# Feed-forward second product in seven block products with pre-summed operands, and a Silu gate

## Chip, core and metric

One core of one Trainium2 chip runs the whole block in one launch. The metric is device time in microseconds (us) of that core. The kernel before takes 2396.96 us (median of three runs, 2396.28 to 2398.84). The engines are TensorE (PE; its weight loads are PEld), VectorE (DVE), ScalarE (ACT), GpSimd (POOL) and SyncE (SP), whose queue issues nearly all transfers.

## The reference, cut to what matters

The block computes token mixing with two recurrent branches, a cross-attention into 256 memory tokens, and a SwiGLU feed-forward, on 1024 tokens of width 1024, all in float32. The feed-forward's inner width is 2816.

```python
h = h + (gate_a * y_a + gate_b * y_b) @ w_out[l]
u = rmsnorm(h, norm_xa_g[l])
...
h = h + o @ xa_wo[l]
u = rmsnorm(h, norm_ffn_g[l])
h = h + (jax.nn.silu(u @ ffn_w1[l]) * (u @ ffn_w3[l])) @ ffn_w2[l]
return rmsnorm(h, norm_final_g)
```

The change is about the last product, hidden (1024 x 2816) by ffn_w2 (2816 x 1024), called part two here, and about the silu in the first two products, called part one.

## The kernel before, in words

Every float32 product is made of three matmuls: each operand is split into a rounded high part (an ACT copy, L281) and the remainder (a subtraction on POOL or DVE, L285), and `mm3` (L298 to L301) adds high by high, high by low and low by high into one PSUM tile.

The mixing stage comes first. Then `attention_block` (L1646) runs, in this order: the keys and values, the output projection of the mixing (`add_project` with w_out, L1763), the queries and attention per head (L1830), and the projection with xa_wo (L1846) in two halves of the tokens. `add_project` (L1706) takes the weights in four passes of 256 columns. In a pass it works through steps of two token tiles, 48 matmuls of 256 columns a step; w_out has sixteen steps, each half of xa_wo has eight. Its weights are loaded by `load_w` as four raw tiles a pass and split into six buffers per part (L1648, L1668), so a part of the next pass can only be split while the last step of the pass before is running. After some steps it calls `next(beside)`, which lets a generator add work there.

Part one (L1957 to L2019) is already a seven-product form over halves of the width (1024) and of the inner width. `products(f, A)` runs for f = 0 to 10; each makes two times seven block products (for ffn_w1 and ffn_w3), of 12 matmuls of 512 columns each. `gated` (L1945) gets the two results of one block, first ffn_w1's (n = 0), then ffn_w3's (n = 1): it takes a Sigmoid on ACT and a product on DVE for the first, and a second product on DVE for the second, and stores the 128 x 512 result in the DRAM tensor hid_d, 44 stores in all.

Part two (L2033 to L2098) goes over two halves of the tokens and two halves of the output columns. For each half of the tokens 22 hidden tiles are loaded and split (L2045 to L2047): the first 14 into the ring (names th, tl), the last eight into the tiles ah, al. For each of the four (token half, column half) pairs all 22 tiles of ffn_w2 are loaded and split (names wh, wl), and four accumulators take 22 x 3 matmuls each. The last three steps are run accumulator by accumulator, so that the sums, the squares and the final norm (L2071 to L2098) follow one another. The remainder of the hidden tiles and that of the weights are both taken on POOL.

What sets the order: in the attention and feed-forward stages a scheduler at build time orders each engine's queue by program order as far as a buffer is free and by its own estimate of readiness; in the queue itself the order is fixed. Loads and stores wait on SP in that order.

Of the kernel before, what the change touches and what calls it, by code (L numbers as in the profile page):

```python
# [17 lines left out]
P = 128  # L18
# [165 lines left out]
def tile_trunk(ctx, tc, x, mem, norm_mix_g, w_in, rw_mu, rw_w0, rw_w2, rw_a0, rw_a2, rw_g2,  # L184
# [1454 lines left out]
    early_d = scratch("early_d", [2, HK, P, HALF])  # L1639
    ssq = const.tile([P, 4, 4], F32, name="ssq")  # L1640
# [5 lines left out]
    def attention_block(xctx):  # L1646
# [27 lines left out]
        Kh = kp.tile([P, KT, NM], F32R, name="Kh")  # L1674
        Kl = kp.tile([P, KT, NM], F32R, name="Kl")
        Vh = vp.tile([P, NMT, D], F32R, name="Vh")
        Vl = vp.tile([P, NMT, D], F32R, name="Vl")
# [28 lines left out]
        def add_project(a, w, src, halves, ss=None, beside=iter(())):  # L1706
# [56 lines left out]
        hs = add_project(yT, w_out, x[0], range(NHALF))  # L1763
# [79 lines left out]
        for _ in prev:  # L1843
            pass

        for h in range(NHALF):  # L1846
            hs = add_project(oT, xa_wo, h1d, range(h, h + 1), *((ssq, early_blocks(hs, *fa)) if h else ()))
# [23 lines left out]
    hd = scratch("hid_d", [FT, NHALF, P, HALF])  # L1871
    def raw(src, k, c, kn, cn):
# [20 lines left out]

    def blocks():

        return [[fp.tile([P, HALF], F32, tag=t, name=f"h{t}", bufs=4 if t == "s" else 2) for t in ts] for ts in (("u2", "u3"), ("c", "s"))
                for _ in range(2)]
# [74 lines left out]
    def early_products(f, T1, T4):  # L1972

        for name, T, b in (("P5", T1, "S1"), ("P4", T4, "B22")):
            for n in range(2):
                t = kept[f, name, n] = fp.tile([P, HALF], F32, tag="kept", name=name, bufs=8)
                nc.scalar.activation(t, product(name, T[n], B[b]), AF.Copy)

    def products(f, A):
# [6 lines left out]
        for n in range(2):  # L1986
# [3 lines left out]
            s = gated(n, C, s, f, 1)  # L1990
        for a11, a12, a21, a22 in A:
# [38 lines left out]
    for f in range(HF):  # L2030
        products(f, weights(f))

    fg = fp.tile([P, D], F32, name="fg", bufs=1)  # L2033
    nc.sync.dma_start(out=fg, in_=norm_final_g.partition_broadcast(P))
    order = [f + e for f in range(HF) for e in (0, HF)]
    ILAST = 3
    for h in range(NHALF):
        a = act(act1)
        hid = []
        for n, f in enumerate(order):  # L2040
            if n >= FT - KT:
                hh, hl = (t[:, n - FT + KT, :] for t in a)
            else:
                hh, hl = (ring.tile([P, HALF], F32R, tag=t, name=t) for t in ("th", "tl"))
            nc.sync.dma_start(out=hl.bitcast(F32), in_=hd[f, h])  # L2045
            nc.scalar.activation(hh, hl.bitcast(F32), AF.Copy)
            nc.gpsimd.tensor_tensor(hl, hl.bitcast(F32), hh.bitcast(F32), op=ALU.subtract)  # L2047
            hid.append((hh, hl))
        hs = blocks()
        for i in range(4):  # L2050
            for c in range(2):
                nc.sync.dma_start(out=hs[i][c], in_=h2d[(4 * h + i) * P:(4 * h + i + 1) * P, c * HALF:(c + 1) * HALF])
        ss = sp.tile([P, 4, 8], F32, tag="ssf", name="ssf")
        for c in range(2):
            cs = slice(c * HALF, (c + 1) * HALF)
            acc = [psum("acc") for _ in range(4)]
            w2 = []
            for n, f in enumerate(order):
                w2.append(operand(raw(ffn_w2, f, c * HALF, 1, HALF), "2"))
                if n < FT - ILAST:  # L2060
                    steps = [(i, n) for i in range(4)]
                elif n == FT - 1:
                    steps = [(i, g) for i in range(4) for g in range(FT - ILAST, FT)]
                else:
                    steps = []
                for i, g in steps:
                    ts_ = slice(i * P, (i + 1) * P)
                    mm3(acc[i], hid[g][0][:, ts_], hid[g][1][:, ts_], w2[g][0][:, 0, :], w2[g][1][:, 0, :],
                        g == 0, g == FT - 1)

            sums = []  # L2071

            def finish(i):

                r = ss[:, 3, i:i + 1]
                o1, o2 = hs[i]
                rows = slice((4 * h + i) * P, (4 * h + i + 1) * P)
                nc.scalar.activation(o1, o1, AF.Copy, scale=r)
                nc.sync.dma_start(out=out[rows, 0:HALF], in_=o1)
                ins = nc.vector.scalar_tensor_tensor(o2, o2, r, fg[:, HALF:D], op0=ALU.mult, op1=ALU.mult).ins  # L2080
                behind(ins, sums[-1])
                nc.sync.dma_start(out=out[rows, HALF:D], in_=o2)

            for i in range(4):
                o = hs[i][c]
                r = [ss[:, n, i:i + 1] for n in range(4)]
                sums.append(nc.vector.tensor_tensor(o, acc[i], o, op=ALU.add).ins.name)  # L2087
                junk = sp.tile([P, HALF], mybir.dt.bfloat16, tag="junkf", name="junkf", bufs=2)
                nc.scalar.activation(junk, o, AF.Square, accum_out=r[c])
                if c == 0:  # L2090
                    nc.gpsimd.tensor_tensor(o, o, fg[:, cs], op=ALU.mult)
                    nc.vector.tensor_scalar(r[0], r[0], 1.0 / D, EPS, op0=ALU.mult, op1=ALU.add)
                else:
                    nc.vector.scalar_tensor_tensor(r[2], r[1], 1.0 / D, r[0], op0=ALU.mult, op1=ALU.add)
                    nc.gpsimd.tensor_tensor(r[3], r[2], nhalf[:, 0:1], op=ALU.pow)
                    if i:
                        finish(i - 1)
        finish(3)  # L2098


# [24 lines left out]
```

## Time and profile before

| what | value |
|---|---|
| runs | 2396.28, 2396.96, 2398.84 us |
| the profiled execution's own time | 2398.55 us |
| its span | 2396.8 us |
| TensorE busy | 97% of the span, granted clock 0.99 on average |
| VectorE, ScalarE, GpSimd busy | 59%, 47%, 51% |

Matmuls are pipelined, so a matmul's duration in the trace (0.39 us for 512 columns) is longer than the distance from one start to the next. In the windows a busy share of PE says how much of a stretch was covered, and idle time in front of a matmul is named with what ended it.

### The profile page before, as it was taken

The numbers are of one execution on the slowest core, as the hardware profiler recorded it, in microseconds if no ns is written. First come the engines' busy times: TensorE is split into PE (matmuls) and PEld (weight loads), VectorE is DVE, ScalarE is ACT, GpSimd is POOL, SyncE is SP. The second block draws the span as 40 slices with busy tenths as digits, with TensorE's granted clock in tenths as the row PEclk, the third lists the DMA queues.
The fourth block names the chain that finished last, engine by engine and source line by source line (L and its number), as shares of the span: only waits on it lengthen the run. The fifth ranks groups of instructions, "written<-read, shape, count | busy, mean of one in ns | idle before, by whom it ended". The sixth has DMA issues, their size and how long they took to land. (4 is left out here: it accounts for less than half of the span.)

```text
span 2396.8 us, 48780 instructions
## 1 busy us (share of the span) xinstructions
PE 2335.8 (97%) x19258; PEld 1934.3 (81%) x19258; DVE 1411.2 (59%) x2288; ACT 1128.3 (47%) x2249; POOL 1228.8 (51%) x1268
## 2 busy tenths in 40 slices
PE   7999999999999999999998999999999999999998
PEld 5777777778887878888887998889778888877887
DVE  5887874667777667767754525444687565640101
ACT  6545454646566656555663415444433333343332
POOL 3554545555466555665664511112565444477673
PEclk9999999999999999999999999999999999999999
DMA  5444445333344343434244823133723223265441
GB/s 168 122 127 121 123 117 161 74 101 85 92 109 110 82 129 105 123 89 126 56 140 152 300 69 117 53 120 132 259 80 101 84 75 93 71 199 172 158 161 57
DMA packets 386001, 288.46 MB, mean 120 GB/s; under 512 B 106171, under 2 KB 329517, under 8 KB 385773
## 3 DMA queue, kind: packets, MB, share of 16 engines
q1 hardware_dynamic: 383341, 279.58, 39.6%
q0 software_dynamic: 1344, 4.72, 0.5%
q8 instruction: 152, 2.49, 0.4%
q10 hardware_dynamic: 1088, 1.05, 0.1%
q14 instruction: 76, 0.62, 0.1%
HBM read 208.73 MB, written 76.02 MB: 119 GB/s over the span
## 5 line engine op out<-in xcount | busy, mean ns | idle before, releaser
L102 PE MATMUL pproj<-uh,whi 128*128 128x512 f32 x768 | 320.0, 417 | 1.1 <-DVE q L102 1.1
L102 PE MATMUL pproj<-uh,wlo 128*128 128x512 f32 x768 | 300.9, 392 | 2.8 <-POOL wlo L102 2.1
L102 PE MATMUL pproj<-ul,whi 128*128 128x512 f32 x768 | 301.2, 392 | 0.0
L285 POOL TENSOR_TENSOR wl<-wraw,wh 128x512 fp32r<-128x512 f32 x154 | 202.1, 1323 | 133.2 <-ACT wh L281 131.6
L285 POOL TENSOR_TENSOR wlo<-wraw,whi 128x512 fp32r<-128x512 f32 (+1 forms) x86 | 117.9, 1374 | 288.6 <-ACT whi L281 280.7
L102 POOL TENSOR_TENSOR wlo<-wraw,whi 128x512 fp32r<-128x512 f32 x96 | 129.0, 1355 | 118.8 <-ACT whi L102 103.8
L281 ACT ACTIVATE whi<-wraw 128x512 fp32r<-128x512 f32 (+1 forms) x166 | 101.0, 617 | 173.1 <-PE pw L301 62.0
L299 PE MATMUL pproj<-uh,whi 128*128 128x512 f32 (+1 forms) x432 | 179.5, 416 | 0.9 <-ACT whi L281 0.6
L281 ACT ACTIVATE wh<-wraw 128x512 fp32r<-128x512 f32 x154 | 94.3, 627 | 182.2 <-PE P L300 74.5
L301 PE MATMUL pproj<-uh,wlo 128*128 128x512 f32 (+1 forms) x432 | 171.4, 397 | 1.5 <-POOL wlo L285 1.5
L102 PEld LDWEIGHTS pproj<-uh,whi 128*128 128x128 f32 x768 | 144.4, 188 | 34.3 <-DVE q L102 2.4
L300 PE MATMUL pproj<-ul,whi 128*128 128x512 f32 (+1 forms) x432 | 170.7, 395 | 0.0
L102 PEld LDWEIGHTS pproj<-ul,whi 128*128 128x128 f32 x768 | 144.3, 188 | 32.0
L102 PEld LDWEIGHTS pproj<-uh,wlo 128*128 128x128 f32 x768 | 144.9, 189 | 28.1 <-POOL wlo L102 2.5
L285 POOL TENSOR_TENSOR wlT<-wraw,whT 128x512 fp32r<-128x512 f32 x70 | 96.6, 1386 | 96.2 <-ACT whT L281 92.5
L299 PE MATMUL pw<-whi,ah 128*128 128x256 f32 x512 | 144.6, 282 | 0.0
L300 PE MATMUL pw<-wlo,ah 128*128 128x256 f32 x512 | 144.6, 282 | 0.0
L301 PE MATMUL pw<-whi,al 128*128 128x256 f32 x512 | 144.3, 282 | 0.0
L2087 DVE TENSOR_TENSOR hu<-acc,hu 128x512 f32<-128x512 f32 x8 | 5.5, 692 | 200.0 <-PE acc L301 200.0
L285 DVE TENSOR_TENSOR wlo<-wraw,whi 128x512 fp32r<-128x512 f32 x80 | 73.7, 922 | 83.4 <-ACT whi L281 83.1
L102 ACT ACT_TABLE_LOAD x90 | 115.5, 1283 | 13.5 <-DVE m L102 6.4
L299 PEld LDWEIGHTS pproj<-uh,whi 128*128 128x128 f32 (+1 forms) x432 | 81.6, 189 | 25.4 <-issue 6.2
(457 smaller groups left out, 6656.2 us busy)
## 6 DMA issues: line engine op xcount, KB each, us to landing
wraw<-in_ffn_w_dram SPq DMA_DIRECT2D x192, 256.0 KB
wraw<-in_w_in_dram SPq DMA_DIRECT2D x148, 256.0 KB
hid_d<-s SPq DMA_DIRECT2D x44, 256.0 KB
tok<-in_x_dram SPq DMA_DIRECT2D x16, 512.0 KB
ar_d<-AR SPq DMA_DIRECT2D x32, 256.0 KB
bk_d<-BK SPq DMA_DIRECT2D x16, 512.0 KB
AR<-ar_d SPq DMA_DIRECT2D x64, 128.0 KB
BK<-bk_d SPq DMA_DIRECT2D x16, 512.0 KB
```

The lines of the kernel that those rows point to most:

```text
L102: r = getattr(self.engine, op)(*a, **kw)
L281: nc.scalar.activation(hi, src, AF.Copy)
L285: e.tensor_tensor(lo, src, hi.bitcast(F32), op=ALU.subtract)
L299: nc.tensor.matmul(ps, ah, bh, start=first, stop=False)
L300: nc.tensor.matmul(ps, ah, bl, start=False, stop=False)
L301: nc.tensor.matmul(ps, al, bh, start=False, stop=last)
L2087: sums.append(nc.vector.tensor_tensor(o, acc[i], o, op=ALU.add).ins.name)
```

## The change

The hidden matrix X is cut into X11, X21 (token half 0 and 1, first eleven inner tiles) and X12, X22 (second eleven), ffn_w2 into four blocks Y likewise. Seven block products replace the eight of before; they need four sums of X blocks and four sums of Y blocks.

- The sums of ffn_w2 (`w2_sums`) are made for each of the eleven f in the attention stages: two loads of 512 KB, two subtractions on DVE, two on POOL, one store of 1 MB to wsum_d. Seven f are placed beside the w_out projection, in the buffers of act2, from its third step on; four beside the first half of xa_wo, in the buffers of the keys and values.
- The sums of the hidden blocks (`hidden_sums`) are made in part one: for each f two operations on DVE, two on POOL and four stores to hsum_d. 33 of the 44 hidden tiles are still stored.
- `gated` takes Silu on ACT in place of Sigmoid and a product on DVE. The gate tiles share a ring of 14 with the kept products (before: rings of 4 and 8).
- Part two runs seven blocks of eleven items. An item loads one hidden (or sum) tile and one weight (or sum) tile, eight items ahead, splits both four items ahead (the hidden remainder on DVE, the weight's on POOL), and feeds twelve matmuls. The block results are combined on ACT and DVE. All hidden tiles now go through the ring; the tiles ah, al hold the sixteen residual tiles, loaded at its start.

```diff
+        def w2_sums(fs, places):
...
+            def sums(f, y):
+                y11, y12, y21, y22 = (y[:, n, :] for n in range(4))
+                nc.vector.tensor_tensor(y11, y12, y11, op=ALU.subtract)
+                nc.gpsimd.tensor_tensor(y12, y22, y12, op=ALU.subtract)
+                nc.gpsimd.tensor_tensor(y22, y22, y11, op=ALU.subtract)
+                nc.vector.tensor_tensor(y21, y22, y21, op=ALU.subtract)
+                nc.sync.dma_start(out=wsd[f], in_=y)
+
+            loaded = []
+            for place in places:
+                if place:
+                    y = place()
+                    f = next(fs)
+                    load(f, y)
+                    loaded.append((f, y))
+                    if len(loaded) < 3:
+                        yield
+                        continue
+                if loaded:
+                    sums(*loaded.pop(0))
+                yield
...
-                    if c > 1 or c == 1 and i2 % 2:
+                    if every or c > 1 or c == 1 and i2 % 2:
                         next(beside, None)
...
-        hs = add_project(yT, w_out, x[0], range(NHALF))
+        hs = add_project(yT, w_out, x[0], range(NHALF), every=True, beside=w2_sums(
+            w2f, [None, None] + [in_act2(tag, n) for tag in ("ah", "al", "ah") for n in range(2)] + [in_act2("al", 0)]))
...
+                             **({} if h else dict(beside=w2_sums(w2f, in_kv), every=True)))
...
         if n == 0:
-            s = fp.tile([P, HALF], F32, tag="s", name="s", bufs=4)
-            nc.scalar.activation(s, C, AF.Sigmoid)
+            s = fp.tile([P, HALF], F32, tag="kept", name="s", bufs=14)
+            nc.scalar.activation(s, C, AF.Silu)
+            return s
         nc.vector.tensor_tensor(s, C, s, op=ALU.mult)
         if n:
-            nc.sync.dma_start(out=hd[f, t], in_=s)
+            hid[f, t] = s
+            if (f, t) != (f % HF, 1):
+                nc.sync.dma_start(out=hd[f, t], in_=s)
...
+    def hidden_sums(f):
+        x11, x21, x12, x22 = (hid.pop(k) for k in ((f, 0), (f, 1), (f + HF, 0), (f + HF, 1)))
+        tt(x22, x21, x22, op=ALU.add)
+        nc.gpsimd.tensor_tensor(x21, x11, x21, op=ALU.subtract)
+        tt(x11, x22, x11, op=ALU.subtract)
+        nc.gpsimd.tensor_tensor(x12, x12, x11, op=ALU.subtract)
+        for n, t in enumerate((x22, x11, x21, x12)):
+            nc.sync.dma_start(out=hsd[n, f], in_=t)
...
+        if f:
+            hidden_sums(f - 1)
...
+    hidden_sums(HF - 1)
...
-            nc.gpsimd.tensor_tensor(hl, hl.bitcast(F32), hh.bitcast(F32), op=ALU.subtract)
...
+    ILAST, LOOK, LOADS = 3, 4, 8
+    blocks = ((lambda f: hd[f, 0], w2(0, 0), p1),
+              (lambda f: hd[f + HF, 0], w2(1, 0), lambda i, acc: add(0, i, 0, acc, ALU.add, True)),
+              (lambda f: hsd[1, f], wsum(3), p6),
+              (lambda f: hsd[0, f], wsum(0), p5),
+              (lambda f: hsd[3, f], w2(1, 1), lambda i, acc: add(0, i, 1, acc, ALU.add, False)),
+              (lambda f: hsd[2, f], wsum(1), p7),
+              (lambda f: hd[f + HF, 1], wsum(2), lambda i, acc: add(1, i, 0, acc, ALU.subtract, False)))
...
+    def split_item(b, f):
+        hl, y = loaded.pop((b, f))
+        hh = ring.tile([P, HALF], F32R, tag="th", name="th")
+        nc.scalar.activation(hh, hl.bitcast(F32), AF.Copy)
+        tt(hl, hl.bitcast(F32), hh.bitcast(F32), op=ALU.subtract)
+        ops[b, f] = (hh, hl, *operand(y, "2"))
...
+    for n, (b, f) in enumerate(items):
+        if n + LOADS < len(items):
+            load_item(*items[n + LOADS])
+        if n + LOOK < len(items):
+            split_item(*items[n + LOOK])
```

## Rows read from the trace of the kernel before

**Rows 1.** The page: the span, and part 1, busy time of each engine.
```profile
span 2396.8 us, 48780 instructions
PE 2335.8 (97%) x19258; PEld 1934.3 (81%) x19258; DVE 1411.2 (59%) x2288; ACT 1128.3 (47%) x2249; POOL 1228.8 (51%) x1268
```
**Rows 2.** Windows: stretch, length, busy time (count) per engine, granted clock, DMA share, GB/s.
```profile
1360.00:1454.00 94.00, 93.95 (x784) 93.72 (x782) 32.23 (x52) 23.30 (x41) 21.04 (x15) 1.00 0.39 136
...
1594.00:1644.00 50.00, 49.67 (x407) 48.11 (x406) 20.25 (x37) 15.03 (x29) 9.67 (x7) 1.00 0.49 165
...
1800.00:2139.00 339.00, 339.00 (x1484) 278.47 (x1483) 202.79 (x260) 116.06 (x192) 179.30 (x137) 1.00 0.31 98
2139.00:2200.00 61.00, 54.21 (x231) 42.64 (x230) 13.11 (x12) 19.57 (x35) 46.84 (x37) 1.00 0.64 207
2200.00:2390.00 190.00, 189.84 (x829) 155.59 (x827) 19.38 (x37) 61.06 (x115) 114.33 (x94) 1.00 0.37 120
```
**Rows 3.** Timeline of PE, starts 24 and 33 matmuls apart, in two stretches.
```profile
2133.84 0.39 PE L299 MATMUL P<-hS,wh 128*128 128x512 f32 x1
...
2139.30 0.39 PE L299 MATMUL acc<-wh,th 128*128 128x512 f32 x1
...
2375.03 0.39 PE L299 MATMUL acc<-wh,ah 128*128 128x512 f32 x1
...
2382.71 0.39 PE L299 MATMUL acc<-wh,ah 128*128 128x512 f32 x1
```
**Rows 4.** PE timeline, 2144 to 2185 us: the matmuls that waited, in brackets.
```profile
2144.85 0.50 PE L299 MATMUL acc<-wh,th 128*128 128x512 f32 x1 [3.35 <-DVE C L2010]
...
2164.72 0.51 PE L300 MATMUL acc<-wl,th 128*128 128x512 f32 x1 [1.94 <-POOL wl L285]
...
2168.46 0.50 PE L300 MATMUL acc<-wl,th 128*128 128x512 f32 x1 [0.68 <-POOL wl L285]
...
2183.43 0.50 PE L300 MATMUL acc<-wl,th 128*128 128x512 f32 x1 [0.68 <-POOL wl L285]
```
**Rows 5.** Timelines of DVE and POOL at the turn to part two.
```profile
2137.13 6.47 DVE L1950 TENSOR_TENSOR s<-C,s 128x512 f32<-128x512 f32 x1 [10.19 <-ACT s L1949]
...
2138.04 2.55 POOL L2047 TENSOR_TENSOR tl<-tl,th 128x512 fp32r<-128x512 f32 x2
2140.52 2.52 POOL L285 TENSOR_TENSOR wl<-wraw,wh 128x512 fp32r<-128x512 f32 x2
```
**Rows 6.** Groups, 2139 to 2397 us: busy, mean ns, idle before, releaser.
```profile
L285 POOL TENSOR_TENSOR wl<-wraw,wh 128x512 fp32r<-128x512 f32 x86 | 110.5, 1300 | 47.9 <-ACT wh L281 46.4 <-issue 1.4
...
L281 ACT ACTIVATE wh<-wraw 128x512 fp32r<-128x512 f32 x84 | 51.1, 625 | 90.5 <-PE acc L301 71.9 <-DMA wraw<-in_ffn_w_dram 8.5 <-POOL wl L285 3.9
```
**Rows 7.** Timelines of POOL and DVE, splits at a pass boundary of w_out.
```profile
1382.60 3.01 POOL L285 TENSOR_TENSOR wlo<-wraw,whi 128x512 fp32r<-128x512 f32 x2 [12.68 <-ACT whi L281]
...
1383.22 1.23 DVE L285 TENSOR_TENSOR wlo<-wraw,whi 128x512 fp32r<-128x512 f32 x1 [4.23 <-ACT whi L281]
...
1385.03 1.12 DVE L285 TENSOR_TENSOR wlo<-wraw,whi 128x512 fp32r<-128x512 f32 x1
```
**Rows 8.** Windows of 10 us with much traffic, the same columns as rows 2.
```profile
1370.00:1380.00 10.00, 10.00 (x86) 10.00 (x85) 2.73 (x7) 0.00 (x0) 0.00 (x0) 1.00 0.98 371
2150.00:2160.00 10.00, 9.89 (x44) 7.91 (x43) 3.04 (x3) 6.63 (x13) 6.64 (x6) 1.00 0.88 276
```
**Rows 9.** Groups of part one, 1698 to 2139 us.
```profile
L285 POOL TENSOR_TENSOR wl<-wraw,wh 128x512 fp32r<-128x512 f32 x68 | 91.5, 1352 | 85.3 <-ACT wh L281 85.2
...
L1950 DVE TENSOR_TENSOR s<-C,s 128x512 f32<-128x512 f32 x43 | 47.5, 1106 | 20.4 <-ACT s L1949 19.8
...
L1993 DVE TENSOR_TENSOR T<-wraw 128x512 f32<-128x512 f32 x22 | 20.9, 948 | 41.8 <-POOL wl L285 41.8
...
L1949 ACT ACTIVATE s<-C 128x512 f32<-128x512 f32 x22 | 13.9, 631 | 29.3 <-DVE C L2010 22.8 <-DVE C L1989 6.2 <-DMA wraw<-in_ffn_w_dram 0.3
...
L1949 ACT ACT_TABLE_LOAD x1 | 1.3, 1283 | 0.0
```

More of the change, by code (lines that the diff above doesn't have):

```diff
@@ L1704, in attention_block, with load, add_project @@
             nc.sync.dma_start(out=t[:, 0:KEYS, :].bitcast(F32), in_=kd[n])
-        def add_project(a, w, src, halves, ss=None, beside=iter(())):
+        def w2_sums(fs, places):
+            def load(f, y):
+                for r in range(2):
+                    rows = slice((f + r * HF) * P, (f + r * HF + 1) * P)
+                    nc.sync.dma_start(out=y[:, 2 * r:2 * r + 2, :].rearrange("p c t -> p (c t)"), in_=ffn_w2[0, rows, :])
+            def sums(f, y):
[18 more added lines that the diff above has]
+                yield
+            for l in loaded:
+                sums(*l)
+                yield
+        def add_project(a, w, src, halves, ss=None, beside=iter(()), every=False):
             hs = []
@@ L1844, in attention_block @@
             pass
+        in_kv = [lambda p=p, t=t: p.tile([P, 4, HALF], F32, tag=t, name="y2")
+                 for p, t in ((kp, "Kh"), (kp, "Kl"), (vp, "Vh"), (vp, "Vl"))]
         for h in range(NHALF):
-            hs = add_project(oT, xa_wo, h1d, range(h, h + 1), *((ssq, early_blocks(hs, *fa)) if h else ()))
+            hs = add_project(oT, xa_wo, h1d, range(h, h + 1), *((ssq, early_blocks(hs, *fa)) if h else ()),
+                             **({} if h else dict(beside=w2_sums(w2f, in_kv), every=True)))
             for i in range(4):
@@ new lines, in tile_trunk, with add @@
+    U = [fp.tile([P, HALF], F32, tag=("u2", "u3")[i // 2], name="Uw") for i in range(4)]
+    V = [fp.tile([P, HALF], F32, tag="kept", name="Vw", bufs=14) for i in range(4)]
+    ss = [sp.tile([P, 4, 8], F32, tag="ssf", name="ssf") for _ in range(NHALF)]
+    sums = {}
+    def add(h, i, c, acc, op, first):
+        o = hs[h][:, 2 * i + c, :]
+        r = [ss[h][:, n, i:i + 1] for n in range(4)]
+        sums[h, i] = (nc.vector.tensor_tensor(o, o, acc, op=op) if op == ALU.subtract else tt(o, acc, o, op=op)).ins.name
+        junk = sp.tile([P, HALF], mybir.dt.bfloat16, tag="junkf", name="junkf", bufs=2)
+        nc.scalar.activation(junk, o, AF.Square, accum_out=r[0 if first else 1])
+        if first:
+            nc.gpsimd.tensor_tensor(o, o, fgs[c], op=ALU.mult)
+            nc.vector.tensor_scalar(r[0], r[0], 1.0 / D, EPS, op0=ALU.mult, op1=ALU.add)
+        else:
+            nc.vector.scalar_tensor_tensor(r[2], r[1], 1.0 / D, r[0], op0=ALU.mult, op1=ALU.add)
+            nc.gpsimd.tensor_tensor(r[3], r[2], nhalf[:, 0:1], op=ALU.pow)
+            if i:
+                finish(h, i - 1, c, sums[h, i])
+            if i == 3:
+                finish(h, 3, c, None)
@@ new lines, in finish @@
+    def finish(h, i, c, order):
+        r = ss[h][:, 3, i:i + 1]
+        rows = slice((4 * h + i) * P, (4 * h + i + 1) * P)
+        o1, o2 = hs[h][:, 2 * i + 1 - c, :], hs[h][:, 2 * i + c, :]
+        if h == 0:
+            nc.vector.tensor_scalar(o1, o1, r, None, op0=ALU.mult)
+        else:
+            nc.scalar.activation(o1, o1, AF.Copy, scale=r)
+        nc.sync.dma_start(out=out[rows, (1 - c) * HALF:(2 - c) * HALF], in_=o1)
+        ins = nc.vector.scalar_tensor_tensor(o2, o2, r, fgs[c], op0=ALU.mult, op1=ALU.mult).ins
+        if order:
+            behind(ins, order)
+        nc.sync.dma_start(out=out[rows, c * HALF:(c + 1) * HALF], in_=o2)
@@ new lines, in more, with p1, p6, p5 @@
+    def more(h, i, c, t):
+        o = hs[h][:, 2 * i + c, :]
+        tt(o, o, t, op=ALU.add)
+    later = []
+    def p1(i, acc):
+        nc.scalar.activation(U[i], acc, AF.Copy)
+        later.append((0, i, 0, U[i]))
+    def p6(i, acc):
+        tt(U[i], acc, U[i], op=ALU.add)
+    def p5(i, acc):
+        tt(V[i], acc, U[i], op=ALU.add)
+        later.append((0, i, 1, V[i]))
+        later.append((1, i, 1, V[i]))
+    def p7(i, acc):
+        tt(U[i], acc, U[i], op=ALU.add)
+        later.append((1, i, 0, U[i]))
+        add(1, i, 1, acc, ALU.add, True)
@@ new lines, in tile_trunk, with load_item @@
+    items = [(b, f) for b in range(len(blocks)) for f in range(HF)]
+    loaded, ops, acc = {}, {}, None
+    def load_item(b, f):
+        t = ring.tile([P, HALF], F32R, tag="tl", name="tl")
+        nc.sync.dma_start(out=t.bitcast(F32), in_=blocks[b][0](f))
+        loaded[b, f] = t, blocks[b][1](f)
+    def split_item(b, f):
[4 more added lines that the diff above has]
+        ops[b, f] = (hh, hl, *operand(y, "2"))
@@ new lines, in tile_trunk @@
+    for item in items[:LOADS]:
+        load_item(*item)
+    for item in items[:LOOK]:
+        split_item(*item)
+    for n, (b, f) in enumerate(items):
[3 more added lines that the diff above has]
+            split_item(*items[n + LOOK])
+        if f == 0:
+            acc = [psum("acc") for _ in range(4)]
+        if f < HF - ILAST:
+            steps = [(i, f) for i in range(4)]
+        elif f == HF - 1:
+            steps = [(i, g) for i in range(4) for g in range(HF - ILAST, HF)]
+        else:
+            steps = []
+        for i, g in steps:
+            hh, hl, yh, yl = ops[b, g]
+            ts_ = slice(i * P, (i + 1) * P)
+            mm3(acc[i], hh[:, ts_], hl[:, ts_], yh[:, 0, :], yl[:, 0, :], g == 0, g == HF - 1)
+        if later:
+            more(*later.pop(0))
+        if f == HF - 1:
+            for i in range(4):
+                blocks[b][2](i, acc[i])
```

97 lines of the change are left out of this document (32 added, 65 removed).

## The prediction

> **What bounds the kernel now.** I read the page first: TensorE is busy for 2335.8 of 2396.8 us, the next engine for 59% [rows 1]. Then the windows by stage, to see whether PE is full where the change works. It is: in the w_out projection (1360 to 1454 us) and the first half of xa_wo (1594 to 1644) PE is covered to 99%, with the DMA engines at 39% and 49%; in part one from 1800 on it has no gap at all; in part two it loses 6.8 of the first 61 us and then runs full [rows 2]. So time is lost or gained in two ways only: matmuls that vanish, and new gaps in front of matmuls. Last the timelines, for what a matmul costs: 24 starts take 5.46 us where the stationary operand comes from the ring, 0.2275 us each, and 33 take 7.68 us in the steps that read ah, al, 0.2327 us each [rows 3]. The printed 0.39 us is a duration in a pipeline and is not used.
>
> **The sum** is made against the profiled execution's own 2398.55 us, 1.6 us above the median of the runs.
>
> *Part two's matmuls.* Before: 4 x 22 x 4 x 3 = 1056. Fourteen of 22 steps read the ring, 672 x 0.2275 = 152.9 us; eight read ah, al, 384 x 0.2327 = 89.4 us; together 242.3. After: 7 x 11 x 4 x 3 = 924, all from the ring, 210.2 us. This is **-32.1 us**, and since PE is the path there it comes out whole if nothing else ends last.
>
> *Can the others keep up?* An item is 12 matmuls, 2.73 us. ACT makes two copies, 1.25 us at 0.625 [rows 6]. POOL makes one remainder, 1.30 us [rows 6], where before it made both, 2.6 us an item, in the first pass over each token half. DVE makes the hidden remainder; the nearest rows with operands in SBUF are 0.95 and 1.11 us [rows 9]. SP moves two tiles of 0.262 MB; at 276 GB/s [rows 8] that is 1.90 us. All lie under 2.73. Over the stage 77 x 0.524 = 40.4 MB of items, 4.2 MB of residuals and 4.2 MB of output in some 217 us ask for 225 GB/s. The first stretch of part two moved 207, and 276 and 371 have been seen [rows 2, 8]. It is tighter than anything after 2200 us before (120 GB/s), but under. The loads run eight items, 22 us, ahead. I cost it at nothing.
>
> *DVE and POOL together.* One DVE product took 6.47 us, where its kind takes 1.1, while POOL ran its operations without a gap until 2143.0 us [rows 5, 9]; the two clearly shut each other out on operands in SBUF. The other view is a burst of two POOL and two DVE splits that took 1382.60 to 1386.15, 3.55 us, or 1.78 us a pair [rows 7]. One pair an item then fits in 2.73 with 0.95 to spare. [...]
>
> *The turn to part two.* Before, PE waited 3.35 + 1.94 + 0.68 + 0.68 = 6.65 us there [rows 4]. The last three are ended by POOL; the first falls where DVE stood in the 6.47 us row, with the PSUM tiles not yet emptied. Both come from POOL having two remainders an item, and POOL now has one. Against it: the residuals, 4.2 MB in eight loads, are all asked for at once when ah, al come free; the last hidden tiles and sums, seven stores of 0.262 MB, sit in the same queue; and the last `hidden_sums` overwrites a tile whose store must land first, with DVE's splits queued behind that wait. Together 6.0 MB, 22 us at 276 GB/s, against 22 us of loads ahead; PE waits for whatever overruns. Bounds: all 6.7 us regained, or 14 us lost (about the 4.2 MB alone, 15 us). I take **-2 us**, nearer the good end, because the named releaser is the one that is relieved.
>
> *Weight sums in the attention stages.* Eleven f, each with 2.1 MB and two operations each on DVE and POOL. Busy time is no matter: POOL is at 22% in w_out and DVE at 34% [rows 2], and an f adds some 2.7 us (POOL, at 1.35) and 1.9 to 2.2 us (DVE) [rows 9] every 5.9 us. What matters is the pass boundary: the splits of a new pass come in one burst just as the pass starts [rows 7], because their buffers come free only then. A sum queued ahead of a burst holds it by up to its POOL pair, 2.7 us, and PE waits for what exceeds its small lead. There are six such boundaries (three in w_out, three in the first half of xa_wo): 0 to 16 us. SP is passed too: 22 loads and 11 stores are queued among those of the weights. I take **+4 us**: half the boundaries hit, by half the pair, since PE has the first parts of the pass to work on meanwhile.
>
> *Part one.* The Silu saves 44 DVE products at 1.11 us, 48 us of DVE [rows 9], and the hidden sums add 22 operations each to DVE and POOL, about 21 and 30 us, and 33 more stores, 8.7 MB or 20 GB/s on top of 98 [rows 2]. PE has no gap from 1800 on with DVE at 60% and POOL at 53%, so gain and cost both vanish under it: **0**. If PE's cover were gone, DVE would gain 27 us and POOL lose 30. The Silu itself I price as the Sigmoid, 0.631 us and one table load of 1.283 us [rows 9]; no row shows a Silu on this path, so the bounds are a load at every change of function, 88 x 1.283 = 113 us of ACT, and none at all. I take the one load, the row nearest in kind.
>
> *The end.* The last norm keeps its chain: 0.
>
> Sum: -32.1 - 2 + 4 = -30.1, so 2368.5 us on the profiled execution's scale and **2367** on that of the median.
>
> **Rivals.**
>
> *Part two starves at its start or its block ends.* For it: six block ends now where three were, all loads on one queue, 225 GB/s. Against it: the lead of eight items and the 371 GB/s seen. At the rate of the old first stretch (207) the 48.8 MB would take 236 us instead of 217: 2367 + 19 = 2386 at worst, some 2378 in the middle. Chance 0.14.
>
> [...] If each pair takes 1.30 + 1.11 = 2.41 us in turn, 77 pairs are 186 us; twelve additions on DVE (13 us) and eight products on POOL (10 us) bring it to 209, as long as PE's 210, and every bunching would be seen: +8 us, 2375. [...] Rows 7 speak against, since there pairs overlap. Chance 0.08.
>
> *A clean turn and no hit at the boundaries.* -32.1 - 6.7: 2358. Chance 0.10.
>
> *The Silu does not do what it should,* and its table is loaded again and again. ACT would go from 34% to about 60% of part one, with splits up to 2.6 us late; some 10 us: 2377. Chance 0.03.
>
> *Slower: the weight sums push the attention stages' own transfers back.* 23.1 MB take 84 us at 276 GB/s; the DMA engines have 94 x 0.61 + 50 x 0.51 = 83 us idle in the two stretches [rows 2], so it fits only if the order on SP lets every load of weights and tokens through in time. It decides when over 30 us of the 84 lie ahead of a load that PE waits for, in the w_out passes above all, where seven f fall: then 2400 and more. Against it: the sums come after the third step in program order, and w_out's weights are loaded well ahead. Chance 0.12, of which 0.05 ends within 0.2% and 0.07 above.
>
> **The numbers.** The forecast as summed holds the remaining 0.53, some 2361 to 2373. A measurement of this kernel can tell 0.2%, 5 us, from no change. Faster by more than that is all but the last rival: 0.88; the same 0.05; slower 0.07. The range reaches up to the starving case at its worst, 2386, and down to 2356; it leaves out the last rival and little else.
>
> **What would show it.** Right: 924 accumulator matmuls at 0.2275 us from start to start; part one as long as before (441 us) with 44 fewer DVE products; less than 7 us of PE gaps after the turn, and those ended by a transfer; gaps of a microsecond or two at w_out's pass boundaries. Wrong: gaps in part two ended by transfers or by DVE splits at each block end; table loads among the Silu rows; or the w_out stage longer than its 94 us by ten or more.

## The result, and the profile after

The changed kernel takes **2383.70 us** (median of four runs, 2380.37 to 2385.71) against 2396.62 for the kernel before: a ratio of 0.9943, 95% interval 0.9926 to 0.9960. It is faster by 13 us, where 30 were forecast. The time lies inside the range given; the size of the gain does not hold.

Where the time went is read first by stage, in the one profiled execution of each kernel, from the first and last matmul of the tiles that mark each stage. All entries are in us, from times rounded to 0.1. The forecast's row is the one before with the prediction's terms; e9 is the best of the variants below.

| kernel | keys to queries (w_out lies in it) | queries to the end of xa_wo | part one | part two | span |
|---|---|---|---|---|---|
| before | 135.3 | 243.9 | 441.0 | 250.1 | 2396.8 |
| after | 139.0 | 250.6 | 438.2 | 224.6 | 2380.1 |
| forecast | 137.3 | 245.9 | 441.0 | 216.0 | |
| best variant (e9) | 135.7 | 245.5 | 439.6 | 209.2 | 2357.2 |

The attention stages grew by 3.7 + 6.7 = 10.4 us where +4 was forecast (half in each stage). Part two shrank by 25.5 where 34.1 was forecast (32.1 and 2). Part one moved by 2.8 where 0 was forecast.

The first column needs a caution. From w_out's first matmul to the first of the queries it is 93.6 us before and 101.1 after, 7.5 more; the column shows only 3.7 of it, because the stretch ahead of w_out took 3.8 us less. There the kernel before ran at a granted clock of 0.50 for 6.8 us (1348.0 to 1354.9), and the kernel after did not. The windows of before, then of after, with the granted clock as the third number from the end:

```profile
1345.00:1358.00 13.00, 10.06 (x61) 9.81 (x61) 8.30 (x8) 6.50 (x13) 8.20 (x6) 0.74 0.73 241
1345.00:1358.00 13.00, 11.10 (x89) 10.49 (x87) 8.23 (x9) 6.99 (x14) 9.57 (x7) 1.00 0.78 269
```

The page of the kernel after, its span and busy times (before: [rows 1]):

```profile
span 2380.1 us, 48890 instructions
PE 2311.5 (97%) x19126; PEld 1913.0 (80%) x19126; DVE 1515.4 (64%) x2397; ACT 1136.1 (48%) x2271; POOL 1235.6 (52%) x1257
```

The windows of the stretches of [rows 2] in the kernel after, the last one cut at the end of part two's matmuls. PE is no longer full in w_out, in xa_wo, nor late in part two; the stretch from 2139 to 2200, which lost 6.8 us before, is now full (part two begins in it, at 2147.5):

```profile
1360.00:1454.00 94.00, 89.40 (x729) 88.79 (x728) 40.19 (x62) 17.41 (x30) 36.20 (x26) 0.98 0.77 274
1594.00:1644.00 50.00, 46.18 (x329) 43.38 (x328) 24.85 (x42) 13.61 (x28) 18.73 (x14) 0.93 0.72 264
1800.00:2139.00 339.00, 339.00 (x1484) 278.34 (x1483) 212.85 (x263) 109.80 (x187) 193.14 (x142) 1.00 0.36 115
2139.00:2200.00 61.00, 61.00 (x269) 50.22 (x268) 38.88 (x40) 30.20 (x53) 35.89 (x25) 1.00 0.85 310
2200.00:2372.00 172.00, 162.78 (x693) 132.31 (x693) 84.50 (x108) 65.75 (x127) 87.37 (x67) 0.97 0.44 147
```

The PE timeline of the kernel after, the matmuls in these stages that waited longest and did not wait before. In brackets is how long PE waited and what ended it:

```profile
1383.59 0.39 PE L300 MATMUL pw<-wlo,ah 128*128 128x256 f32 x1 [2.08 <-POOL wlo L285]
1385.82 0.45 PE L300 MATMUL pw<-wlo,ah 128*128 128x256 f32 x1 [1.25 <-DVE wlo L285]
...
1411.27 0.39 PE L299 MATMUL pw<-whi,ah 128*128 128x256 f32 x1 [1.26 <-DVE tok L1758]
...
1634.61 0.39 PE L300 MATMUL pw<-wlo,ah 128*128 128x256 f32 x1 [2.47 <-POOL wlo L285]
1636.84 0.58 PE L300 MATMUL pw<-wlo,ah 128*128 128x256 f32 x1 [1.01 <-DVE wlo L285]
...
2292.64 0.49 PE L299 MATMUL acc<-wh,th 128*128 128x512 f32 x1 [1.26 <-ACT wh L281]
2293.99 0.80 PE L300 MATMUL acc<-wl,th 128*128 128x512 f32 x1 [0.85 <-POOL wl L285]
2332.10 0.80 PE L299 MATMUL acc<-wh,th 128*128 128x512 f32 x1 [5.91 <-ACT wh L281]
```

These places carry it: a pass boundary in w_out (1384) and, less, the next one (1411), one in xa_wo (1635), and the last three items of blocks five and six in part two (2290, 2332).

**The pass boundary.** The POOL timeline of the kernel after, at xa_wo:

```profile
1630.71 1.29 POOL L1718 TENSOR_TENSOR y<-y 128x512 f32<-128x512 f32 x1 [2.07 <-DVE y L1717]
1632.08 1.26 POOL L1719 TENSOR_TENSOR y<-y 128x512 f32<-128x512 f32 x1
1633.30 2.94 POOL L285 TENSOR_TENSOR wlo<-wraw,whi 128x512 fp32r<-128x512 f32 x2
```

ACT's rounded copies of the new pass run from 1628.71 to 1631.33 and POOL had nothing to do from 1628.64 on, but its two sums of the weights (L1718, L1719) stand ahead of the two remainders that PE waits for. It is the picture that the prediction drew, with two differences. The sums hold the burst by more than their own 2.6 us, because the first of them waits 2.07 us for DVE's sum. And behind the gap the matmuls themselves are slow, at a granted clock of 0.50. The windows of that stretch show it, the clock being the third number from the end:

```profile
1630.00:1634.00 4.00, 2.14 (x19) 1.94 (x18) 1.26 (x3) 1.29 (x3) 3.21 (x3) 1.00 0.64 262
1634.00:1638.00 4.00, 2.37 (x11) 2.08 (x12) 4.00 (x5) 0.00 (x0) 2.23 (x2) 0.65 0.57 199
1638.00:1642.00 4.00, 4.00 (x21) 4.00 (x20) 0.05 (x1) 0.00 (x0) 0.00 (x0) 0.50 0.98 290
1642.00:1646.00 4.00, 4.00 (x37) 4.00 (x37) 0.76 (x2) 0.00 (x0) 0.00 (x0) 1.00 1.08 381
```

From 1638 to 1642 PE is busy all the time and starts 21 matmuls instead of 37: the granted clock is 0.50, where it was 1.00 from 1630 to 1634 and is 1.00 again from 1642 on. It fell at 1635.1, half a microsecond after the wait of 2.47 us had ended, from where on the starts of the 256-column matmuls lie 0.21 us apart instead of 0.11, and it stayed down past the second wait. The stage grew by 6.7 us, of which the two gaps are 3.5.

**Part two.** Windows of 10 us; a full one has 46 matmuls:

```profile
2290.00:2300.00 10.00, 7.46 (x24) 5.38 (x24) 1.97 (x3) 3.45 (x6) 3.15 (x4) 0.83 0.53 177
...
2310.00:2320.00 10.00, 9.79 (x43) 7.56 (x42) 9.09 (x13) 5.83 (x13) 6.35 (x7) 1.00 0.61 206
2320.00:2330.00 10.00, 6.20 (x28) 4.80 (x26) 4.17 (x3) 0.00 (x0) 3.63 (x3) 1.00 0.59 193
2330.00:2340.00 10.00, 7.34 (x20) 5.47 (x21) 6.63 (x8) 5.73 (x11) 6.21 (x5) 0.66 0.43 153
```

Missing are 22 + 3 + 18 + 26 = 69 starts; at 0.2264 us (209.2 us over 924 matmuls, in the variant without gaps) that is 15.6 us, and 224.6 - 209.2 is 15.4. PE's idle time is 9.2 us of it. Of the other 6, some 3.2 are 16 starts behind the gaps that lie 0.42 to 0.43 us apart instead of 0.23, at a granted clock of 0.50 (2295 to 2297 and 2334 to 2338); the rest lies in the starts next to the gaps.

Why PE waited is on ACT. Its timeline around the long gap:

```profile
2316.52 1.66 ACT L281 ACTIVATE wh<-wraw 128x512 fp32r<-128x512 f32 x3
2330.90 0.63 ACT L2200 ACTIVATE th<-tl 128x512 fp32r<-128x512 f32 x1 [12.72 <-DMA tl<-hid_d]
2331.44 0.61 ACT L281 ACTIVATE wh<-wraw 128x512 fp32r<-128x512 f32 x1
```

A hidden copy (th) waited 12.72 us for its transfer, and the weight copy (wh) that PE needed stood behind it in ACT's queue. That copy itself waited for nothing once its turn came, and counted row by row its tile is the one that SP asked for at 2296.72, 35 us before. The groups of part two (2130 to 2390) say that hidden copies wait for transfers all through it:

```profile
L281 ACT ACTIVATE wh<-wraw 128x512 fp32r<-128x512 f32 x79 | 47.4, 618 | 15.9 <-PE acc L301 12.8 <-POOL wl L285 3.1
...
L2200 ACT ACTIVATE th<-tl 128x512 fp32r<-128x512 f32 x72 | 44.9, 630 | 94.8 <-DMA tl<-hsum_d 54.8 <-DMA tl<-hid_d 39.1 <-DVE tl L2201 0.5
```

ACT stands idle for 94.8 us in front of hidden copies, nearly all of it ended by transfers. The change as written splits both tiles of an item four items ahead; counted row by row, ACT's queue has the hidden copies up to 13 items ahead of the weight copies from block five on (nine at the long gap), so each meets a load issued only a few microseconds before. What made one of them 12.7 us late is on SP: the eight output stores of the first token half, issued between 2310.25 and 2322.50 as their data came, ahead of the load:

```profile
2296.72 0.32 SPq L2176 DMA_DIRECT2D wraw<-wsum_d  x1
...
2322.50 0.33 SPq L2146 DMA_DIRECT2D out_dram<-hres  x1
2322.93 2.43 SPq L2176 DMA_DIRECT2D wraw<-wsum_d  x3
2325.45 0.38 SPq L2194 DMA_DIRECT2D tl<-hid_d  x1
```

### The profile page after: what moved, and what is told of

Same layout as the page of the kernel before. It is cut to its first block, busy times and chain, and to the rows that moved or that the text cites. A ratio compares the mean times of both kernels' runs of the same rounds, so it can differ in the third digit from the quotient of the medians.

```text
span 2380.1 us, 48890 instructions
## 1 busy us (share of the span) xinstructions
PE 2311.5 (97%) x19126; PEld 1913.0 (80%) x19126; DVE 1515.4 (64%) x2397; ACT 1136.1 (48%) x2271; POOL 1235.6 (52%) x1257
## 3 DMA queue, kind: packets, MB, share of 16 engines
q8 instruction: 151, 2.47, 0.4%
## 5 line engine op out<-in xcount | busy, mean ns | idle before, releaser
L285 POOL TENSOR_TENSOR wl<-wraw,wh 128x512 fp32r<-128x512 f32 x143 | 202.0, 1427 | 153.3 <-ACT wh L281 139.9
L102 PEld LDWEIGHTS pproj<-uh,whi 128*128 128x128 f32 x768 | 144.4, 188 | 34.1 <-DVE q L102 2.0
L299 PE MATMUL acc<-wh,th 128*128 128x512 f32 x308 | 121.5, 395 | 7.2 <-ACT wh L281 7.2
L2201 DVE TENSOR_TENSOR tl<-tl,th 128x512 fp32r<-128x512 f32 x77 | 77.1, 1028 | 79.1 <-ACT th L2200 75.2
L281 ACT ACTIVATE wh<-wraw 128x512 fp32r<-128x512 f32 x143 | 86.4, 622 | 82.5 <-PE P L300 57.3
L300 PE MATMUL acc<-wl,th 128*128 128x512 f32 x308 | 122.2, 397 | 2.0 <-POOL wl L285 2.0
```

The source lines that it names most:

```text
L102: r = getattr(self.engine, op)(*a, **kw)
L281: nc.scalar.activation(hi, src, AF.Copy)
L285: e.tensor_tensor(lo, src, hi.bitcast(F32), op=ALU.subtract)
L299: nc.tensor.matmul(ps, ah, bh, start=first, stop=False)
L300: nc.tensor.matmul(ps, ah, bl, start=False, stop=False)
L2201: tt(hl, hl.bitcast(F32), hh.bitcast(F32), op=ALU.subtract)
```

## The experiments

Each is an edit of the kernel after; the stages are again those of one profiled execution each. Theory A: the weight sums cost by operations queued ahead of the splits at pass boundaries. Theory B: they cost by their transfers. Theory C: part two loses by the output stores on SP ahead of the loads. Theory D: it loses because hidden tiles and weight tiles get out of step; in a first form the loads were to be put in step, in the second (D2) the copies on ACT.

| run | median us | ratio to before, 95% | keys to queries | to end of xa_wo | part one | part two |
|---|---|---|---|---|---|---|
| e1, sums left out | 2372.78 | 0.9899 (0.9884, 0.9913) | 135.4 | 245.4 | 440.3 | 221.2 |
| e2, sums on DVE | 2370.16 | 0.9887 (0.9872, 0.9901) | 135.6 | 245.4 | 438.8 | 221.9 |
| e3, stores last | 2377.43 | 0.9917 (0.9900, 0.9933) | 139.9 | 250.6 | 440.8 | 215.5 |
| e4, loads in step | 2393.16 | 0.9985 (0.9975, 0.9995) | 138.8 | 250.7 | 440.3 | 232.5 |
| e5, Sigmoid again | 2385.86 | 0.9956 (0.9943, 0.9970) | 138.8 | 251.0 | 441.6 | 220.9 |
| e6, copies in step | 2370.44 | 0.9890 (0.9876, 0.9903) | 138.0 | 249.7 | 440.0 | 209.2 |
| e7, e2 + e3 | 2369.91 | 0.9887 (0.9874, 0.9901) | 135.4 | 245.7 | 438.7 | 218.8 |
| e8, e2 + e3 + e6 | 2359.95 | 0.9848 (0.9834, 0.9861) | 135.1 | 245.6 | 440.8 | 209.2 |
| e9, e2 + e6 | 2358.27 | 0.9842 (0.9828, 0.9855) | 135.7 | 245.5 | 439.6 | 209.2 |
| e10, e8 once more | 2359.74 | 0.9846 (0.9832, 0.9859) | 134.8 | 243.9 | 438.9 | 209.2 |

**e1: the sums' transfers alone**

```diff
-                nc.vector.tensor_tensor(y11, y12, y11, op=ALU.subtract)
-                nc.gpsimd.tensor_tensor(y12, y22, y12, op=ALU.subtract)
-                nc.gpsimd.tensor_tensor(y22, y22, y11, op=ALU.subtract)
-                nc.vector.tensor_tensor(y21, y22, y21, op=ALU.subtract)
```

> The kernel after without the four operations on each ffn_w2 tile; the loads and stores of 23 MB stay, so the last product is computed from unsummed weights. Changed kernel: w_out stage 101.1 us (93.6 before), queries to the end of xa_wo 250.6 us (243.9 before), span 2380.1. Theory A (the sums stand ahead of the weight splits on POOL and DVE at a pass boundary): both stages back to within 2 us of before, 94 to 96 and 244 to 246, span near 2368. Theory B (the transfers push the weight loads back on SP): both stages stay at 101 and 250, span near 2380.

e1 leaves the sums out, so its last product is that of unsummed weights; it is for timing alone. The stages fall to 135.4 and 245.4 us: 3.6 us in the first and 5.2 of the 6.7 in the second are gone while every load and store is still there. The first half of xa_wo, and in it the stretch where the kernel after stood and crawled, in the windows of e1:

```profile
1594.00:1644.00 50.00, 49.67 (x382) 47.52 (x381) 20.22 (x37) 15.79 (x31) 11.26 (x8) 1.00 0.84 320
1634.00:1642.00 8.00, 8.00 (x70) 8.00 (x69) 1.63 (x3) 2.02 (x4) 1.38 (x2) 1.00 1.01 377
```

The DMA engines are busy to 0.84 at 320 GB/s, where [rows 2] had 0.49 and 165, and PE keeps 1.00 of the clock: 70 starts in the eight microseconds in which the kernel after made 11 + 21 = 32. So at this boundary the operations cost and the traffic does not. The 1.5 us left in the second stage are within what the same stage varies by between equal kernels (245.6 in e8, 243.9 in e10). In w_out the case is less clean: from its first matmul to the queries e1 takes 97.7 us, where 94 to 96 were expected and the kernel before had 93.6. The gaps at 1384 are gone altogether, but e1 has 2.3 us of gaps at w_out's start (0.39, 0.96 and 0.96 us, up to 1364.51) that the kernel after does not have. The other variants have 0 to 1.8 us there, with POOL's sums or without them. What causes these was not tried, so a part for the transfers at w_out's start is not excluded.

**e2: POOL's two sums on DVE**

```diff
-                nc.gpsimd.tensor_tensor(y12, y22, y12, op=ALU.subtract)
-                nc.gpsimd.tensor_tensor(y22, y22, y11, op=ALU.subtract)
+                nc.vector.tensor_tensor(y12, y22, y12, op=ALU.subtract)
+                nc.vector.tensor_tensor(y22, y22, y11, op=ALU.subtract)
```

> All four operations of the weight sums on DVE, so that POOL has splits only. Theory A: the POOL part of the gaps at the two bad boundaries (2.1 and 2.5 us, ended by a split on POOL) goes, with it most of the clock's fall; the DVE part may stay or grow by an operation of 0.7 us. w_out 95 to 98, queries to xa_wo 245 to 248, span 2370 to 2376. Theory B: no change, 2380.

All the work is done again, and the stages are as short as without it (97.3 us from w_out's first matmul to the queries). On DVE a sum takes 0.69 us where POOL took 1.3, and nothing stands ahead of POOL's remainders. DVE at the w_out boundary in e2:

```profile
1381.85 0.69 DVE L1720 TENSOR_TENSOR y<-y 128x512 f32<-128x512 f32 x1
1382.55 3.39 DVE L285 TENSOR_TENSOR wlo<-wraw,whi 128x512 fp32r<-128x512 f32 x2
```

PE's gaps at w_out's boundaries shrink to 0.40 us (from 2.08 + 1.25) and 0.58 us (from 1.26), with none in xa_wo; one of 0.96 us stands at w_out's start. Theory A holds at the boundaries, with the queue on POOL as its place. The edit takes away two things at once, POOL's slower sums and POOL's wait for DVE ahead of them; which weighs more was not tried.

**e3: the first half's output stores behind the last load**

```diff
-        nc.sync.dma_start(out=out[rows, (1 - c) * HALF:(2 - c) * HALF], in_=o1)
+        store(h, out[rows, (1 - c) * HALF:(2 - c) * HALF], o1)
...
-        nc.sync.dma_start(out=out[rows, c * HALF:(c + 1) * HALF], in_=o2)
+        store(h, out[rows, c * HALF:(c + 1) * HALF], o2)
...
+        if b == 6 and f > 2:
+            to, t = stores.pop(0)
+            behind(nc.sync.dma_start(out=to, in_=t).ins, last[-1])
```

> The eight output stores of the first token half are queued on SP behind the last load of part two instead of in the middle of block six's loads. Theory C (loads of the next block wait on SP behind stores whose data is late): the gap of 5.9 us at the end of block five goes, and the slow-clock stretch after it, part two 224.6 to 215-218 us; the gaps of 2.5 us near 2290 stay. Theory D (ACT's queue holds the weight copies behind hidden copies whose tile has only just been asked for, whatever the stores do): the 5.9 us gap stays at 4 us or more, part two 222 to 225.

The gap of 5.91 us is gone and part two takes 215.5. Gaps of a microsecond remain, in the middle of block six (item five, at 2316 and 2318) and in its last items, ended by ACT's and POOL's weight splits:

```profile
2316.13 0.50 PE L299 MATMUL acc<-wh,th 128*128 128x512 f32 x1 [1.08 <-ACT wh L281]
...
2331.99 0.49 PE L300 MATMUL acc<-wl,th 128*128 128x512 f32 x1 [0.85 <-POOL wl L285]
```

So the stores have a part in it, but something is left that they do not explain.

**e4: each hidden load behind its item's weight load**

```diff
-        t = ring.tile([P, HALF], F32R, tag="tl", name="tl")
-        nc.sync.dma_start(out=t.bitcast(F32), in_=blocks[b][0](f))
-        loaded[b, f] = t, blocks[b][1](f)
+        w = blocks[b][1](f)
+        t = ring.tile([P, HALF], F32R, tag="tl", name="tl")
+        behind(nc.sync.dma_start(out=t.bitcast(F32), in_=blocks[b][0](f)).ins, issued[-1])
+        loaded[b, f] = t, w
```

> Each hidden load is queued on SP behind the weight load of its own item, so that hidden copies on ACT run 9 instead of 13 items ahead of the weight copies, and a hidden tile's buffer is free well before its load comes up. Theory D: the gaps near 2290 (2.5 us) go and the 5.9 us one shrinks to under 3, part two 214 to 219 us. Theory C: the gaps near 2290 may go, the 5.9 us one stays over 4, part two 219 to 224.

A miss: part two grows to 232.5, with 14.2 us of gaps instead of 9.2. The hidden copies' group in e4 (2125 to 2390) shows why:

```profile
L2203 ACT ACTIVATE th<-tl 128x512 fp32r<-128x512 f32 x74 | 46.4, 631 | 114.0 <-DMA tl<-hsum_d 68.9 <-DMA tl<-hid_d 43.8 <-DVE Vw L2164 0.9
```

The hidden loads came later, but the copies that wait for them stood where they had stood on ACT, in front of the weight copies (mostly 9 items ahead where 13 were). They waited longer, 114.0 us instead of 94.8. With the two streams coupled by ACT's order, delaying the loads of one delayed the other as well.

**e5: the Sigmoid and its product again**

```diff
-            nc.scalar.activation(s, C, AF.Silu)
-            return s
+            nc.scalar.activation(s, C, AF.Sigmoid)
```

> Edit: the gate is a Sigmoid activation and a product on VectorE again, as before the change; all else as after it. The same number of activations of the same shape on ScalarE, and 44 products of 128x512 more on VectorE in part one (0.8 to 1.5 us each, 35 to 65 us of VectorE in 438 us of part one). The prediction's theory (the Silu form is worth nothing, since TensorE sets the pace of part one and a gate has a block product of slack): 2383.7 within 4 us, part one 438 to 441 us. Rival (Silu is worth part of the 13 us that were gained, since the products stand on VectorE among the block sums that part one's operands wait for): part one 445 us or more, 2390 or more. Rival (Silu costs, by a slower activation or a table load): 2379 or less.

2385.86 us against 2383.70: the two intervals overlap, and part one is 3.4 us longer than in the kernel after, 0.8 longer than the longest of the other kernels that have Silu (440.8). In its PE timeline there are two gaps that the kernel after does not have:

```profile
1831.09 0.50 PE L301 MATMUL P<-ah,wlT 128*128 128x512 f32 x1 [0.92 <-POOL wlT L285]
1837.78 0.47 PE L299 MATMUL P<-hS,wh 128*128 128x512 f32 x1 [1.30 <-DVE U L2067]
```

They sum to 2.2 us. By the medians that is too little for these runs to settle, but the profiles are plainer: from the 301st of part one's 1848 matmuls on, it takes 353.98 us in before, after and every variant but e5, where it takes 356.81. So in this one execution the hidden sums beside a Sigmoid cost 2.8 us, and with the Silu they cost nothing. A row of the kernel after prices the Silu: one load of the table, as the Sigmoid had [rows 9], and the activations at 0.633 us each:

```profile
L1993 ACT ACTIVATE s<-C 128x512 f32<-128x512 f32 x21 | 13.3, 633 | 86.0 <-DVE C L2075 45.2 <-DVE C L2052 40.8
...
L1993 ACT ACT_TABLE_LOAD x1 | 1.3, 1283 | 0.0
```

**e6: the weight copy ahead of the hidden copy on ACT**

```diff
         hh = ring.tile([P, HALF], F32R, tag="th", name="th")
-        nc.scalar.activation(hh, hl.bitcast(F32), AF.Copy)
+        y = operand(y, "2")
+        behind(nc.scalar.activation(hh, hl.bitcast(F32), AF.Copy).ins, his[-1])
         tt(hl, hl.bitcast(F32), hh.bitcast(F32), op=ALU.subtract)
-        ops[b, f] = (hh, hl, *operand(y, "2"))
+        ops[b, f] = (hh, hl, *y)
```

(`his` keeps the names of the rounded copies in the order in which `split` makes them.)

> Edit: in part two an item's rounded copy of the hidden tile on ScalarE stands behind the rounded copy of its weight tile, where it runs 13 items ahead of it in the kernel after the change; loads and their order as after the change. Theory D2 (ScalarE's order couples the two streams: a hidden copy that waits for its transfer, 12.72 us of waiting at the end of block five, holds weight copies whose data has long come, so the two gaps of 1.3 and 5.9 us at the ends of blocks four and five are ended by ScalarE's copies): without the coupling the gap of 5.9 us at 2332 goes and part two takes 224.6 - 8 to 224.6 - 5 = 217 to 220 us, the whole 2376 to 2379. Theory C alone (the loads come late on SP, behind the output stores, and whatever order ScalarE keeps, their tiles come late): within 2 us of 2383.7, with gaps of the same size. Rival (as with the hidden loads put behind the weight loads, a short lead makes a ring of waits): part two 230 us or more, 2389 or more.

Part two takes 209.2 us, without a single gap, although the loads and the stores stand on SP as in the kernel after. The loads' and stores' order on SP is the same but for a few neighbours that changed places. The gain is 8 us more than D2 itself had asked for, since the small gaps and the clock's fall went with the large one: the granted clock is 1.00 in every window of e6 from 2120 to 2358. The two groups in e6 (2130 to 2390):

```profile
L283 ACT ACTIVATE wh<-wraw 128x512 fp32r<-128x512 f32 x78 | 49.0, 629 | 91.3 <-POOL wl L287 54.2 <-issue 24.1 <-PE P L302 5.9
L2203 ACT ACTIVATE th<-tl 128x512 fp32r<-128x512 f32 x77 | 47.3, 616 | 4.1 <-DMA tl<-hid_d 4.1
```

Hidden copies wait 4.1 us for transfers where they waited 94.8. ACT's idle time now stands in front of the weight copies; the profile puts more than half of its end down to POOL's remainders and has no transfer among the three largest causes.

**e7 and e8: the mends together**

> Edit: both mends together: the two weight sums of each item that ran on GpSimd run on VectorE, and the eight output stores of the first half of the rows stand behind the last load of part two on SP's queue. The two theories speak of different stages (the attention stages and part two), so the gains should add: by the stage table queries to part one as with the sums on VectorE (135.6 and 245.4 us), part two as with the stores last (215.5), the whole 2370.2 - 6.3 = 2363.9, within 4 us. If the granted clock or the layout of the buffers ties the stages, it falls short of that by over 4 us: 2368 or more.

> Edit: sums on VectorE, output stores last, and the weight copy ahead of the hidden copy in ScalarE's order. Theory C with D2 (the gaps of 1 us that are left at the ends of blocks four to six with the stores last are ScalarE's order): part two 213 us or less, the whole 2361 or less. If only the queue on SP mattered: as with the two mends, 2364 within 3 us. If the short lead makes a ring: 2370 or more.

e7 misses: 2369.91 us, where the sum was 2364, and no better than e2 alone. Its attention stages are as in e2; its part two takes 218.8, where e3 had 215.5. As long as ACT's order couples the streams, part two comes out anywhere between 215.5 and 224.6 us in kernels whose part two differs in the stores at most (e1, e2, e3, e5, e7 and the kernel after). With the weight copy first it is 209.2 every time, and e8 takes 2359.95.

**e9 and e10: are the stores needed as a cause?**

> Edit: as the run with both mends and the weight copy first, but the output stores stand again where the change has them, between the loads of part two. Theory D2 alone (ScalarE's order is the whole cause in part two, the late stores only one of the things that make a hidden tile late): part two 209 to 210 us without a gap, the whole 2360 within 3 us. Theory C also (the stores on SP cost by themselves once ScalarE's order is mended): part two 212 us or more, 2363 or more.

> Edit: none against the run with both mends and the weight copy first; it is run beside the one without the stores moved, on the same chip, so that the two can be compared. Both theories: 2360 within 2 us, part two 209 us.

e9 leaves the stores where the change has them and takes 2358.27 us, e10 beside it on the same chip 2359.74, and the two ranges overlap. The stores cost nothing that these runs can tell once a late hidden tile no longer holds the weight copies. The windows of e9 in the stages of [rows 2], with PE full in both halves of part two:

```profile
1594.00:1644.00 50.00, 49.67 (x394) 48.02 (x393) 29.80 (x51) 14.32 (x29) 10.33 (x7) 1.00 0.87 321
...
2140.00:2200.00 60.00, 60.00 (x266) 49.68 (x265) 36.19 (x33) 27.59 (x52) 34.03 (x25) 1.00 0.86 308
2200.00:2349.00 149.00, 149.00 (x659) 123.36 (x658) 106.88 (x109) 65.80 (x126) 88.37 (x63) 1.00 0.48 157
```

e9 beats both kernels: by the medians it is 39 us under the one before, and 25 under the one after, which was not run beside it.

## Why the prediction was right and wrong

**Part two's matmuls, -32.1: right.** There are 924, and without gaps they take 209.2 us (210.2 forecast).

**The turn, -2: right in kind, too small.** PE has no gap from the first accumulator matmul at 2147.5 on until 2290; all 6.65 us of [rows 4] are regained, as the prediction's better bound had it. The releaser named there, POOL, is the one that was relieved; that this alone did it was not tried. The eight residual loads, which made up the other bound, cost nothing.

**"Can the others keep up?", with "I cost it at nothing": this step failed.** Each engine does have less than 2.73 us of work an item (in e6 two copies of 0.62 and 0.63 us on ACT, 1.46 on POOL, 1.36 on DVE), and e6 and e9 run without a gap on part two's same work, loads and stores. What it left out is the order in which one engine serves two streams. ACT's queue is fixed at build time; in the kernel after a hidden copy at its head waited 12.72 us for a transfer, and ACT did nothing in that time, with the weight copy that PE needed next in its queue. The sentence "The loads run eight items, 22 us, ahead" covers a late load only if the copies stand in the order in which PE needs them. It cost 15.4 us, 9.2 of them idle. The prediction's sign of being wrong was gaps at block ends, ended by transfers or DVE splits; the gaps came, but 7.2 us of them are ended by ACT's copies and the rest by POOL's remainders, with the late transfer one step further back, as the 12.72 us row and e6 show.

The rival of block ends named the places (gaps at the block ends) and about the price (2378 in its middle), but not the mechanism. It made the total rate of the transfers the bound, and its remedy would have been less traffic or an earlier load. e6 and e9 move as much in less time.

**The weight sums, +4: the mechanism was right, this term was mis-sized; it measured 10.4 us.** "A sum queued ahead of a burst holds it by up to its POOL pair" is what the rows at 1630.71 to 1633.30 show, and e1 and e2 confirm it at the boundaries; SP and the DMA engines had room there, as the prediction argued against its slower rival. Three boundaries at 1.35 us each were forecast. Three were hit, but with 2.08 + 1.25, 1.26 and 2.47 + 1.01 us of gaps. The four sums form a chain over two engines: POOL's first waits for DVE's, and DVE's last waits for POOL's (5.87 us ahead of 1382.34 at w_out) with DVE's share of the remainders behind it, so PE waits twice at a boundary.

The other part of it has no term in the sum at all. "So time is lost or gained in two ways only: matmuls that vanish, and new gaps in front of matmuls" leaves out the granted clock, which was 0.65 and then 0.50 in the windows behind the gap at 1635: there 3.5 us of gaps became 6.7 us. That the first column shows 3.7 us and not 7.5 is luck, the slow stretch in the kernel before.

**Part one, 0: right, and for the reason given.** From its 301st matmul on it takes 353.98 us before and after. The 2.8 us lie ahead of that, in the first 300 matmuls: 87.0 us before, 84.2 after, and 84.8 to 86.9 in the variants, though the code of part one differs in e5 alone. Gain and cost did not quite both vanish under PE's cover: e5 says that the hidden sums without the Silu cost 2.8 us.

**DVE and POOL in turn, and the Silu table,** did not decide. In e6 a pair of remainders takes 1.46 + 1.36 = 2.82 us, more than an item if taken in turn. But in the windows of e9 from 2140 to 2349 DVE is busy for 143.1 and POOL for 122.4 of 209 us, so their rows overlap, and PE has no gap there. That the two shut each other out is the prediction's reading of one row [rows 5]; how far one held the other up was not tried. And there is one table load.

**The sum.** By stage it is +3.7 + 6.7 - 2.8 - 25.5 = -17.9, and -16.7 by the spans, with small shifts ahead of the keys and at the end. By the medians it is -12.9: the profiled execution of after lies 1.9 us under its median, that of before 1.9 over its own. With both losses mended, e9 comes out at 2358.27, where the prediction's clean case said 2358. There is some luck in so close a fit: by stage e9 has -40.9 in part two, -1.4 in part one and +2.0 before it, where the clean case had -38.8 and nothing else. But part two's gains were read correctly, and what failed are the two costs: nothing for keeping up in part two (15.4 us) and 4 us for the weight sums (10.4 us).

## What to carry to other kernels

When two streams go through one engine's fixed queue, compare not only the busy time an item needs with the pace of the bottleneck, but also the order of the streams in that engine's queue: look for an operation that waits for a transfer ahead of one whose data has long come, and put the operation that the bottleneck needs next first (here 15 us of part two for one swapped pair of copies). Put added work on an engine whose queue has no urgent operation just behind it. Look in the old trace for gaps in front of TensorE with a lower granted clock behind them, and where there are some, price a new gap at more than its length (here 1.6 to 1.9 times).

## What the runs showed of the hardware that was not expected

A gap cost up to 1.9 times its length here: 3.5 us of gaps lost 6.7 us in xa_wo, 3.3 us lost 5.4 at 1384, and 9.2 us lost 15.4 in part two. After the gaps at 2292.64 and 2293.99 the accumulator matmuls start 0.42 to 0.43 us apart, and from 2297.47 on 0.23 apart again, for the same shape:

```profile
2295.01 0.63 PE L299 MATMUL acc<-wh,th 128*128 128x512 f32 x1
2295.43 0.63 PE L300 MATMUL acc<-wl,th 128*128 128x512 f32 x1
...
2297.47 0.39 PE L299 MATMUL acc<-wh,th 128*128 128x512 f32 x1
2297.70 0.39 PE L300 MATMUL acc<-wl,th 128*128 128x512 f32 x1
```

The granted clock differs with the spacing: it is 0.50 in the window from 2295 to 2297 and 1.00 from 2297.47 to 2310. In the kernel before, the gaps at the turn (3.35 us, then 1.94 and 0.68) left the clock at 1.00 in the windows around them, so not every gap brought it down. Why it fell behind some and not behind others was not tried. The effect could have been seen before the change: in part one of the kernel before a gap of 2.69 us is followed by a granted clock of 0.50 (1754.3 to 1757.4), and the window around it shows 0.72:

```profile
1753.12 0.50 PE L300 MATMUL P<-lS,whT 128*128 128x512 f32 x1 [2.69 <-DVE lS L285]
1752.00:1758.00 6.00, 4.88 (x14) 3.87 (x15) 4.83 (x7) 4.07 (x6) 6.00 (x5) 0.72 0.00 1
```
